# Four-product chains in a transformer trunk: the third and fourth token sums made inside the first chain

## The chip, the cores and the metric

The kernel runs on one core of one Trainium2 chip. Its metric is device time in microseconds, the median of several executions. One execution is also taken with a hardware profiler; its trace is what the views below are read from. The engines are named as the profile names them: PE is TensorE (matmuls), PEld its weight loads, DVE VectorE, ACT ScalarE, POOL GpSimd, SP SyncE. Each works through its own queue in the order in which the program wrote it, and waits at an instruction until the semaphores that it names are there.

## The reference

A trunk of two layers over 512 tokens of width 1024. Layer 0 mixes tokens by dilated windowed attention, layer 1 by a gated recurrence; each is followed by a gated convolutional feed-forward network, with norms before and after. What the change touches is that network:

```
def conv_ffn(x, w_up, conv_w, conv_b, w_down):
    u = causal_dwconv(x @ w_up, conv_w, conv_b)      # w_up: 1024 x 6144, 3 taps
    g, v = u[..., :D_FF], u[..., D_FF:]              # D_FF = 3072
    return (jax.nn.gelu(g, approximate=True) * v) @ w_down
```

Everything is float32. The kernel keeps that accuracy by writing each operand as a high part and a remainder in a shorter format, and by three matmuls for each product (high x high, high x low, low x high; `PASSES`, line 336).

## The kernel before, in words

The feed-forward network (`ffn`, line 674) runs twice. The normed input stands transposed in `hT`, features on partitions, 512 tokens in the free dimension. Weights arrive by SyncE in blocks of 256 columns (`load`, line 280, three buffers `raw`). `pump` (line 245) splits a block into `whi` on ScalarE (line 153) and `wlo` on VectorE (line 154), sixteen units being alive at most. A result tile of 128 features x 512 tokens is a sum over eight blocks of features; `conv` (lines 677 to 686) then does the three taps, the first on ScalarE (line 679) and two on VectorE (line 683), and gelu (line 695, ScalarE) or the product with the gate (line 697, VectorE) follow.

For the gate half of columns 3 to 10 (`SEVEN`, line 39) the product is done as a 2 x 2 block product with seven block products in place of eight (`seven`, line 783). Its operands are blocks of the weights, sums of them (lines 205 and 209 on VectorE, and two additions made by GpSimd DMAs, line 191), blocks of `hT`, and four sums of blocks of `hT` over the two token halves. These four token sums are the same for all eight columns. `token_sums` (line 732) makes them once in each layer: `both` (line 746, the addition at 749) adds the high and low parts of a block of `hT` back together, lines 764, 770, 771 and 777 form the differences and sums, and `parted` (line 757) splits each into two pairs of tiles `T`, by two copies on ScalarE (line 153) and two subtractions on VectorE (line 154).

One column of the seven products is a `chain` (line 813). Its steps are laid into slots by `AT` (line 40): first s1 with the first token sum, then, between quarters of another tile, w11, s4, w12, s2 with the second sum, s3 with the third and a22 with the fourth. Eight chains follow each other 15 slots apart. A chain has two accumulators in PSUM. Between steps they are copied and combined: line 836 (ScalarE) copies the first product aside, which the s4 step needs before it adds to the same bank; lines 840 and 841 (ScalarE) copy both accumulators behind s4, which the w12 step waits for; line 845 (VectorE) finishes the first half of the result ahead of s3, line 848 the second ahead of a22. The chains' matmuls are line 830, those of the other tiles line 340.

The order of work is written out by the program. After each tile or slot `tick` (line 303) runs: it advances the side generators, of which `token_sums` is one, and then pumps one or two weight pieces. A `yield n` lets the generator rest until the nth tick from there. What a slot puts off to later slots (`later`) is emitted ahead of the tick. There are seven ticks between the start of `token_sums` and the first slot of `seven`; in the kernel before it is done by the seventh.

Of the kernel before, what the change touches and what calls it, by code (L numbers as in the profile page):

```python
# [78 lines left out]
def kernel(  # L79
# [38 lines left out]
    def nm(s):  # L118
        uid[0] += 1
        return f"{s}{uid[0]}"  # L120

    def gen(dt=F32, s="g"):
        return gp.tile([P, 512], dt, tag="g", name=nm(s))
# [28 lines left out]
    def split(hi, lo, raw):  # L152
        nc.scalar.activation(hi, raw, AF.Copy)  # L153
        nc.vector.tensor_tensor(lo, raw, hi.bitcast(F32), op=ALU.subtract)  # L154
# [519 lines left out]
    def ffn(layer, hT, post, pre):  # L674
# [31 lines left out]
        for j in range(SEVEN[0]):  # L706
            if j == 1:
                side(token_sums(hT, T))
            if j < SEVEN[0] - 1:
                feat_tiles(2, hT, lambda b, ps: sink(b, ps, j), j == 0)  # L710
            else:
                feat_tiles(1, hT, lambda b, ps: sink(b, ps, j))
                i = chunk()
                feat_tile(i, 0, hT, lambda ps: sink(2, ps, j))
# [17 lines left out]
    def token_sums(hT, T):  # L732

        assert len(sides) == 1
        d = dp.tile([P, 4, D], F32, name=nm("x_kept"))
        nc.gpsimd.dma_start(d, X[0])
        kept.append(d)
        homes = cp.tile([P, 4, D], F32R, tag="x_sb", name=nm("T"))
        homes = [homes[:, n] for n in range(4)]
        homes += [cp.tile([P, D], F32R, tag="gain", name=nm("T"), bufs=2) for _ in range(2)]  # L740
        homes = [[h[:, 0:512], h[:, 512:1024]] for h in homes]
        homes += [[gen(F32R, "T") for _ in range(2)] for _ in range(2)]
        homes = [[h.rearrange("p (k t) -> p k t", k=2) for h in hs] for hs in homes]
        yield 1

        def both(k0, n):
            o = gen(s="B").rearrange("p (k t) -> p k t", k=2)
            hi, lo = (h[:, k0 : k0 + 2, n * 256 : n * 256 + 256] for h in hT)
            tt(o, hi.bitcast(F32), lo.bitcast(F32), op=ALU.add)  # L749
            return o  # L750

        tt = nc.vector.tensor_tensor

        def whole(k0, n):
            return [both(k0 + 2 * k, n) for k in range(2)]

        def parted(n, b):
            for k in range(2):
                split(homes[2 * n][k], homes[2 * n + 1][k], b[k])

        b11, b12 = whole(0, 0), whole(0, 1)
        yield 1
        for k in range(2):
            tt(b11[k], b11[k], b12[k], op=ALU.subtract)
        parted(0, b11)
        yield 1
        b22, b21 = whole(4, 1), whole(4, 0)
        yield 1
        for k in range(2):
            tt(b12[k], b12[k], b22[k], op=ALU.subtract)  # L770
            tt(b22[k], b22[k], b11[k], op=ALU.add)
        yield 1
        parted(1, b22)
        parted(2, b12)
        yield 1
        for k in range(2):
            tt(b21[k], b21[k], b22[k], op=ALU.subtract)
        parted(3, b21)
        T.extend([homes[2 * n], homes[2 * n + 1]] for n in range(4))

    LEFT = {5: ("s1", 1), 1: ("w11", 0), 3: ("s4", 1), 2: ("w12", 0), 6: ("s2", 1), 7: ("s3", 1), 4: ("a22", 1)}

# [647 lines left out]
```

## Time and profile before

| what | us |
| --- | --- |
| median of 3 executions | 1456.36 (1455.86 to 1456.72) |
| the profiled execution, its time | 1456.06 |
| its span, first to last instruction | 1454.3 |
| PE busy | 1436.9 (99%) |
| DVE busy | 971.1 (67%) |
| ACT busy | 736.3 (51%) |
| POOL busy | 178.5 (12%) |
| mean granted TensorE clock | 0.995 of full speed |

A row of a timeline has the start in us from the span's begin, the time from the first start to the last end, engine, line, operation, output and inputs by the program's names (buffer numbers left out), the shape and how many in a row; in brackets the idle time of the engine before it and what ended it. A row of waits has the waiting engine and line, whom it waited for, the total in us, how often, and the longest. Matmuls are pipelined, and their ends are modelled.

### The profile page before, as it was taken

The numbers are of one execution on the slowest core, as the hardware profiler recorded it, in microseconds if no ns is written. First come the engines' busy times: TensorE is split into PE (matmuls) and PEld (weight loads), VectorE is DVE, ScalarE is ACT, GpSimd is POOL, SyncE is SP. The second block draws the span as 40 slices with busy tenths as digits, with TensorE's granted clock in tenths as the row PEclk, the third lists the DMA queues.
The fourth block names the chain that finished last, engine by engine and source line by source line (L and its number), as shares of the span: only waits on it lengthen the run. The fifth ranks groups of instructions, "written<-read, shape, count | busy, mean of one in ns | idle before, by whom it ended". The sixth has DMA issues, their size and how long they took to land.

```text
span 1454.3 us, 20563 instructions
## 1 busy us (share of the span) xinstructions
PE 1436.9 (99%) x7437; PEld 1233.1 (85%) x7437; DVE 971.1 (67%) x2115; ACT 736.3 (51%) x1644; POOL 178.5 (12%) x311
## 2 busy tenths in 40 slices
PE   9999999999999998999999999999998999999998
PEld 7888888888888897989988888888897899988886
DVE  6767747474735979777774348769779777764333
ACT  7656636262615555555543335588454555554331
POOL 0441414040402101101000001000100111000000
PEclk9999999999999999999999999999999999999999
DMA  7653637373726253554452322432333545453201
GB/s 224 207 146 110 172 115 212 100 213 99 217 95 211 87 181 85 142 133 107 137 202 89 114 73 87 131 116 87 117 121 110 146 111 145 123 189 116 87 1 58
DMA packets 142846, 189.66 MB, mean 130 GB/s; under 512 B 9312, under 2 KB 119352, under 8 KB 142232
## 3 DMA queue, kind: packets, MB, share of 16 engines
q1 hardware_dynamic: 114280, 145.48, 31.2%
q0 software_dynamic: 27616, 41.82, 12.0%
q8 instruction: 58, 0.95, 0.3%
q10 hardware_dynamic: 848, 1.05, 0.2%
q14 instruction: 44, 0.36, 0.1%
HBM read 168.83 MB, written 19.49 MB: 129 GB/s over the span
## 4 chain that ended last, share of the span: by engine, by line
PE 85%; DVE 8%; ACT 5%; issue 1%; DVEq 0%; ACTq 0%
PE ps L340 37%; PE acc L340 24%; PE ps L830 11%; PE v L1024 8%; DVE wlo L154 2%; DVE u L683 2%; PE v L954 2%; DVE xb L1233 1%; ACT whi L153 1%; PE O L1175 1%; PE S L1120 1%; PE S L1074 1%; DVE B L749 1%; ACT sig L1254 1%; PE O L340 1%
## 5 line engine op out<-in xcount | busy, mean ns | idle before, releaser
L340 PE MATMUL ps<-hT,whi 128*128 128x512 f32 (+1 forms) x2240 | 646.6, 373 | 0.0
L340 PEld LDWEIGHTS ps<-hT,whi 128*128 128x128 f32 x2240 | 405.0, 189 | 68.8
L340 PE MATMUL ps<-hT,wlo 128*128 128x512 f32 (+1 forms) x1120 | 416.3, 372 | 0.0
L154 DVE TENSOR_TENSOR wlo<-raw,whi 128x512 fp32r<-128x512 f32 x408 | 269.4, 688 | 189.6 <-ACT whi L153 189.6
L153 ACT ACTIVATE whi<-raw 128x512 fp32r<-128x512 f32 x408 | 244.4, 627 | 225.1 <-PE acc L340 118.2
L340 PEld LDWEIGHTS ps<-hT,wlo 128*128 128x128 f32 x1120 | 211.6, 189 | 37.4
L340 PE MATMUL acc<-whi,ahi 128*128 128x512 f32 x512 | 199.6, 390 | 0.0
L340 PE MATMUL acc<-whi,alo 128*128 128x512 f32 x512 | 199.3, 389 | 0.1
L340 PE MATMUL acc<-wlo,ahi 128*128 128x512 f32 x512 | 199.2, 389 | 0.0
L147 ACT ACTIVATE whi<-raw,first_w 128x128 fp32r<-128x128 f32 (+1 forms) x432 | 147.1, 427 | 55.3 <-PE ps L340 30.4
L683 DVE SCALAR_TENSOR_TENSOR u<-ps,cols,u 128x511 f32<-128x511 f32 x192 | 143.6, 748 | 42.6 <-ACT u L679 39.2
L148 DVE SCALAR_TENSOR_TENSOR wlo<-raw,first_w,whi 128x128 fp32r<-128x128 f32 (+1 forms) x432 | 139.6, 391 | 1.9 <-ACT whi L147 1.9
L340 PEld LDWEIGHTS acc<-whi,alo 128*128 128x128 f32 x512 | 96.1, 188 | 20.5 <-DVE alo L154 0.6
L340 PEld LDWEIGHTS acc<-wlo,ahi 128*128 128x128 f32 x512 | 96.1, 188 | 19.8
L340 PEld LDWEIGHTS acc<-whi,ahi 128*128 128x128 f32 x512 | 96.1, 188 | 19.8
L679 ACT ACTIVATE u<-ps,cols 128x512 f32<-128x512 f32 x96 | 73.9, 769 | 70.2 <-DVE ps L845 40.0
L1024 PE MATMUL v<-whi,hT 128*128 128x512 f32 x320 | 102.3, 393 | 0.0
L830 PE MATMUL ps<-T,whi 128*128 128x256 f32 x512 | 92.8, 280 | 0.0
L191 POOL DMA_DIRECT2D raw<-in_ffn_w_up_dram x32 | 41.5, 1489 | 375.1 <-DVE wlo L154 215.6
L383 POOL DMA_DIRECT2D turned<-T x36 | 19.7, 549 | 532.8 <-DVE T L377 529.5
L390 POOL DMA_DIRECT2D ft<-turned x144 | 79.1, 557 | 40.2 <-issue 18.0
L830 PEld LDWEIGHTS ps<-T,whi 128*128 128x128 f32 x512 | 80.1, 189 | 1.6
(196 smaller groups left out, 1609.8 us busy)
## 6 DMA issues: line engine op xcount, KB each, us to landing
raw<-in_ffn_w_up_dram SPq DMA_DIRECT2D x48, 1024.0 KB
raw<-in_attn_w_qkv_dram SPq DMA_DIRECT2D x67, 512.0 KB
raw<-in_ffn_w_down_dram SPq DMA_DIRECT2D x24, 1024.0 KB
raw<-in_ffn_w_up_dram POOLq DMA_DIRECT2D x32, 256.0 KB, 4.6
raw<-in_lru_w_in_dram SPq DMA_DIRECT2D x8, 1024.0 KB
turned<-T POOLq DMA_DIRECT2D x28, 256.0 KB, 2.6
ft<-turned POOLq DMA_DIRECT2D x112, 64.0 KB, 6.0
vrows<-v SPq DMA_DIRECT2D x16, 256.0 KB
```

Of the source, the lines that this page charges most:

```text
L147: nc.scalar.activation(hi[:, k], raw[:, k], AF.Copy, scale=w)
L148: nc.vector.scalar_tensor_tensor(lo[:, k], raw[:, k], w, hi[:, k].bitcast(F32), op0=ALU.mult, op1=ALU.subtract)
L153: nc.scalar.activation(hi, raw, AF.Copy)
L154: nc.vector.tensor_tensor(lo, raw, hi.bitcast(F32), op=ALU.subtract)
L191: nc.gpsimd.dma_start(to, src, accum_op=ALU.add)
L340: mm(dst, l[a], r[b], start=start and n == 0, stop=stop and n == 2)
L390: nc.gpsimd.dma_start(t[32 * c : 32 * c + 32].rearrange("j (b x) -> j b x", b=4), d.rearrange("(b j) (c x) -> c j b x", j=32, c=4)[c],)
L679: nc.scalar.activation(u, ps, AF.Identity, scale=cc[:, j : j + 1], bias=cc[:, 48 + j : 49 + j])
L683: nc.vector.scalar_tensor_tensor(u[:, d:], ps[:, : S - d], wc, u[:, d:], op0=ALU.mult, op1=ALU.add)
L830: mm(y[b][:, 0:256], W[wa][0][:, k, :], right[n](ha, k), start=n in (1, 5) and k == q == 0, stop=k == 3 and q == 2, skip_group_check=True,)
L954: mm(banks[t], hT[a][:, k, t * P : (t + 1) * P], W[b][k % 2][:, 0, :], start=u == n == 0, stop=u == 3 and n == 5,)
L1024: mm(banks[t], hT[a][:, k, t * P : (t + 1) * P], W[b][k % 2][:, 0, :], start=(k, a, b) == (0, 0, 0), stop=(k, a, b) == (KD - 1, 1, 0),)
```

## The change

The generator `token_sums` makes the same four sums by the same operations. Their places differ. The block that only the fourth sum needs (`b21`) is made later, the third sum is split inside the chain, and the fourth is formed and split there too. The list `T` of the tiles is filled after the second sum, ahead of the writes of the last two sums.

```
@@ -764,19 +764,22 @@ def token_sums
             tt(b11[k], b11[k], b12[k], op=ALU.subtract)
         parted(0, b11)
         yield 1
-        b22, b21 = whole(4, 1), whole(4, 0)
-        yield 1
+        b22 = whole(4, 1)
         for k in range(2):
             tt(b12[k], b12[k], b22[k], op=ALU.subtract)
             tt(b22[k], b22[k], b11[k], op=ALU.add)
         yield 1
         parted(1, b22)
+        T.extend([homes[2 * n], homes[2 * n + 1]] for n in range(4))
+        yield 5
         parted(2, b12)
+        yield 4
+        b21 = whole(4, 0)
         yield 1
         for k in range(2):
             tt(b21[k], b21[k], b22[k], op=ALU.subtract)
+        yield 1
         parted(3, b21)
-        T.extend([homes[2 * n], homes[2 * n + 1]] for n in range(4))
```

By ticks: the second sum is formed in the fourth tick (fifth before) and split in the fifth (sixth before). The third sum is split in the tick of the chain's third slot, behind the copy of line 836, which the second slot emits (sixth tick before). The block for the fourth sum is made in the tick of the seventh slot, the sum formed in that of the eighth, and split in that of the ninth (fourth and seventh tick before). The instructions of PE, POOL and SP keep their order; on DVE and ACT the moved ones change places with weight splits and convolutions. Lines behind the change have numbers larger by 3.

More of the change, by code (lines that the diff above doesn't have):

```diff
@@ L766, in token_sums @@
         yield 1
-        b22, b21 = whole(4, 1), whole(4, 0)
-        yield 1
+        b22 = whole(4, 1)
         for k in range(2):
@@ L773, in token_sums @@
         parted(1, b22)
+        T.extend([homes[2 * n], homes[2 * n + 1]] for n in range(4))
+        yield 5
         parted(2, b12)
+        yield 4
+        b21 = whole(4, 0)
         yield 1
@@ L777, in token_sums @@
             tt(b21[k], b21[k], b22[k], op=ALU.subtract)
+        yield 1
         parted(3, b21)
-        T.extend([homes[2 * n], homes[2 * n + 1]] for n in range(4))
     LEFT = {5: ("s1", 1), 1: ("w11", 0), 3: ("s4", 1), 2: ("w12", 0), 6: ("s2", 1), 7: ("s3", 1), 4: ("a22", 1)}
```

## The prediction

> **What bounds the kernel now.** I read the page's busy shares first, then the list of waits of TensorE alone, then the timeline around the longest of them.
>
> ```profile
> span 1454.3 us, 20563 instructions
> ...
> PE 1436.9 (99%) x7437; PEld 1233.1 (85%) x7437; DVE 971.1 (67%) x2115; ACT 736.3 (51%) x1644; POOL 178.5 (12%) x311
> ```
>
> ```profile
> PE ps L830 <- ACT part L836: 8.8, 2, 4.4
> ```
>
> TensorE is the bound, busy for 99% of the span. Of all its listed waits one kind is large: line 830, the products of the chains, waited twice (once in each feed-forward layer) for `part` at line 836, the copy of the first chain's first sum; 8.8 us in all. What moves TensorE is worth its full size, and nothing else is worth anything. So the question is what the moved work does to these two places, and what TensorE waits for next.
>
> I number the slots of the first chain as they are emitted: slot 1 is the product with the first token sum (left operand s1), 2 and 3 are quarters of another tile, 4 is the product of w11, 5 is s4, 6 and 7 quarters, 8 is w12, 9 is s2 (second token sum), 10 to 13 quarters, 14 is s3 (third sum), 20 is a22 (fourth sum). TensorE's timeline, at the starts of slots 2, 4, the end of 4, then 5, 8, 9 and 14; then the end of slot 4, slots 5 and 8 of the second layer:
>
> ```profile
> 564.48 0.63 PE L340 MATMUL ps<-hT,whi 128*128 128x512 f32 x2
> ...
> 567.22 0.40 PE L830 MATMUL ps<-hT,whi 128*128 128x256 f32 x2
> ...
> 568.53 0.28 PE L830 MATMUL ps<-hT,wlo 128*128 128x256 f32 x1
> 573.23 0.50 PE L830 MATMUL ps<-hT,whi 128*128 128x256 f32 x2 [4.42 <-ACT part L836]
> ...
> 579.08 0.40 PE L830 MATMUL ps<-hT,whi 128*128 128x256 f32 x2
> ...
> 580.51 0.40 PE L830 MATMUL ps<-T,whi 128*128 128x256 f32 x2
> ...
> 587.41 0.40 PE L830 MATMUL ps<-T,whi 128*128 128x256 f32 x2
> ...
> 1120.72 0.28 PE L830 MATMUL ps<-hT,wlo 128*128 128x256 f32 x1
> 1125.41 0.80 PE L830 MATMUL ps<-hT,whi 128*128 128x256 f32 x2 [4.42 <-ACT part L836]
> ...
> 1131.95 0.39 PE L830 MATMUL ps<-hT,whi 128*128 128x256 f32 x2
> ```
>
> A chain product takes 1.43 us (579.08 to 580.51), two quarters 2.74 (564.48 to 567.22). Matmuls of this width follow each other by 0.12, so slot 5 was due at 568.65 and came at 573.23: 4.58 us lost. Slots 5 to 7 should then take 1.43 + 2.74 = 4.17 and took 5.85 (573.23 to 579.08): 1.68 more. In the second layer it is 4.57 (1120.84 to 1125.41) and 6.54 - 4.17 = 2.37. The second part is the clock:
>
> ```profile
> 567.18:570.60 3.42, 1.63 (x13) 1.39 (x12) 3.26 (x6) 1.00 (x2) 0.00 (x0) 1.00 0.77 254
> 570.60:574.01 3.41, 0.78 (x6) 0.78 (x7) 3.38 (x7) 3.10 (x7) 0.00 (x0) 1.00 0.20 64
> 574.01:577.42 3.41, 3.41 (x13) 3.00 (x12) 2.71 (x6) 1.49 (x3) 1.28 (x1) 0.50 0.89 299
> ...
> 1120.14:1123.56 3.42, 0.86 (x8) 0.65 (x6) 3.29 (x6) 1.78 (x4) 0.00 (x0) 1.00 0.91 303
> 1123.56:1126.97 3.41, 1.55 (x7) 1.56 (x8) 3.38 (x7) 2.32 (x5) 0.00 (x0) 0.50 0.21 52
> ```
>
> Each row is a stretch of time with its length, the busy time of TensorE, of its weight loads and of three other engines, and the granted clock as the third number from the end. The clock is halved behind a stretch with 0.78 us of TensorE work and behind one with 0.86, and not behind one with 1.63. The two stalls cost 4.58 + 1.68 + 4.57 + 2.37 = 13.20 us in all.
>
> **The change.** It adds and removes no instruction; the order changes on VectorE and ScalarE alone. TensorE's, GpSimd's and SyncE's orders stay. In each layer eight VectorE operations (two sums of line 749, two of 777, four splits at 154) and four ScalarE copies (153) leave the stretch ahead of the copy of line 836 for places behind it. The rows of ScalarE, then VectorE:
>
> ```profile
> 562.51 0.63 ACT L695 ACTIVATE u<-u 128x512 f32<-128x512 f32 x1 [3.04 <-DVE u L683]
> 563.04 2.19 ACT L153 ACTIVATE T<-B 128x512 fp32r<-128x512 f32 x4
> ...
> 565.66 0.76 ACT L679 ACTIVATE u<-ps,cols 128x512 f32<-128x512 f32 x1
> 569.60 1.23 ACT L153 ACTIVATE T<-B 128x512 fp32r<-128x512 f32 x2 [3.18 <-DVE B L777]
> 570.74 2.17 ACT L153 ACTIVATE whi<-raw 128x512 fp32r<-128x512 f32 x4
> 572.82 0.36 ACT L836 ACTIVATE part<-ps 128x256 f32<-128x256 f32 x1
> ...
> 575.93 2.19 ACT L153 ACTIVATE whi<-raw 128x512 fp32r<-128x512 f32 x4 [2.23 <-DVE raw L209]
> ...
> 578.42 0.37 ACT L841 ACTIVATE ps<-ps 128x256 f32<-128x256 f32 x1
> ```
>
> ```profile
> 551.37 2.49 DVE L749 TENSOR_TENSOR B<-hT,hT 128x512 f32<-128x512 f32 x4
> 553.77 1.29 DVE L154 TENSOR_TENSOR wlo<-raw,whi 128x512 fp32r<-128x512 f32 x2
> 554.98 1.53 DVE L683 SCALAR_TENSOR_TENSOR u<-ps,cols,u 128x511 f32<-128x511 f32 x2
> 556.42 0.68 DVE L770 TENSOR_TENSOR B<-B,B 128x512 f32<-128x512 f32 x1
> ...
> 560.88 1.53 DVE L683 SCALAR_TENSOR_TENSOR u<-ps,cols,u 128x511 f32<-128x511 f32 x2
> 563.69 2.50 DVE L154 TENSOR_TENSOR T<-B,T 128x512 fp32r<-128x512 f32 x4 [1.28 <-ACT T L153]
> ...
> 568.88 1.29 DVE L777 TENSOR_TENSOR B<-B,B 128x512 f32<-128x512 f32 x2
> 570.26 1.30 DVE L154 TENSOR_TENSOR T<-B,T 128x512 fp32r<-128x512 f32 x2
> 571.47 1.89 DVE L154 TENSOR_TENSOR wlo<-raw,whi 128x512 fp32r<-128x512 f32 x3
> ...
> 575.21 0.69 DVE L209 TENSOR_TENSOR raw<-raw 128x512 f32<-128x512 f32 x1
> ...
> 583.04 0.42 DVE L845 TENSOR_TENSOR ps<-part,ps 128x256 f32<-128x256 f32 x1
> ```
>
> These give the pitch of a VectorE operation, 0.60 (2.40 for four from 551.37 to 553.77), that of a ScalarE copy, 0.52 (2.08 for four from 570.74 to 572.82), and the old chain: VectorE, full of other work, reaches line 777 at 568.88; ScalarE's split of the fourth sum waits for it until 569.60; four weight copies and line 836 stand behind that split; slot 5 stands behind line 836.
>
> *Slot 5.* I step the new order from 551.37. Until the convolution that began at 560.88 VectorE sheds two sums (1.20) and takes up the two splits of the second sum (1.21) with a wait for ScalarE. That turn-round (convolution, ScalarE's activation, ScalarE's split, VectorE's split) took 2.81 from 560.88 to 563.69, where two convolution steps alone hold the queue 1.45 (554.98 to 556.42), so the wait is 1.36. The convolution begins at 562.25. The activation at 695 follows 1.63 behind, as before (560.88 to 562.51), at 563.88. Then, on ScalarE, one weight copy at +0.53, the convolution's first step at +0.52, four weight copies at +0.76 (565.66), line 836 at +2.08: 567.77, done 0.36 later, at 568.13. Slot 5 is due at 568.65, so this stall goes, with 0.5 us to spare; each microsecond by which I am wrong beyond that comes back in each layer.
>
> *Slot 8, what is late next.* Slot 8 waits for line 841, which ScalarE reaches behind four weight copies, the first of which waits for line 209 on VectorE (575.93, above). Up to line 209 VectorE sheds 1.20 for two sums, 1.21 for two splits of the third sum, 1.38 for line 777 with its wait (568.88 to 570.26), 1.21 for two splits of the fourth: 5.00. It takes up a second turn-round of 1.36, since the weight split behind the next convolution has no splits of sums ahead of it now. Line 209 comes 3.64 earlier, at 571.57; line 841 ended 3.58 behind its start (575.21 to 578.79), now at 575.15, and slot 8 begins 0.05 later (573.18 to 573.23 for the old wait), at 575.20. It is due at 568.65 + 4.17 = 572.82. So a new wait of 2.38 us takes the old one's place. From both sides: nothing, if the turn-rounds are hidden, to 4.6, the old wait, if little of the shed time reaches line 209. I take 2.38, since each term has a row in this very stretch.
>
> *Slots 9, 14 and 20.* The second sum is split at about 559, long before slot 9. Slot 14 waits for the third sum, split by 573.5, and for line 845. From line 209 on VectorE has 16 steps at 0.60 (line 209, two splits of the third sum, four of weights, two sums, one weight split, two of line 777, one weight split, two splits of the fourth sum, line 697) and one convolution of 1.45: 11.05 us, so line 845 begins at 582.62 and ends 0.42 later at 583.04, hardly earlier than before (583.46). TensorE needs it at 575.20 + 8.33 (579.08 to 587.41) = 583.53. It is hidden by 0.5 us; without that cover each microsecond is paid in full, in both layers. The fourth sum is split at 582 and used six slots after slot 14. The four ScalarE copies moved (2.1 us) lie in its waits, of 2.23 at 575.93 and the like.
>
> *Transfers.* No issue is moved in its queue, but two wait for VectorE: SyncE's next loads and GpSimd's addition for the second chain.
>
> ```profile
> 566.82 6.33 SPq L280 DMA_DIRECT2D raw<-in_ffn_w_up_dram  x2
> 575.59 1.28 POOL L191 DMA_DIRECT2D raw<-in_ffn_w_up_dram  x1 [23.99 <-DVE wlo L154]
> DMA to landing us min/median/max: 4.4/4.6/5.8
> ```
>
> The first load goes out 1 us earlier, the addition 3.6 (at 572); landed in 5.8 at the worst it is there at 577.8. The weight split that reads it comes behind line 777, at 580.2, and its copy on ScalarE 0.65 ahead, at 579.6: 1.8 us of cover, behind which line 845 would be late by as much. I cost it at nothing.
>
> *Sum.* First layer: slot 8 begins at 575.20 instead of 579.08, 3.88 saved. Second: the same steps put it 6.55 behind 1120.84, at 1127.39 instead of 1131.95, 4.56 saved. Together 8.44. All that follows is TensorE's own work at 99%, so it reaches the end: 1456.06 (the profiled execution: span 1454.3 and 1.8 around it) - 8.44 = 1447.6 us. The median of the runs, 1456.36, is 0.3 above that execution.
>
> **The rivals.** *The clock falls at the new wait.* For it: a gap of 2.2 us (2.38 less the 0.16 that the last matmul runs past its pitch) leaves 1.2 us of work in a stretch of 3.41, if it lies in one; that is between 0.86, which halved the clock, and 1.63, which didn't. Against it: the stretches stand on a fixed grid of 3.41 us in both layers (574.01 to 1123.56 is 161 of them), the gap may lie across a border, and then neither has so little. Price 1.68 to 2.37 a layer: 1449.3 to 1450.0 for one, 1451.7 for both. [...]
>
> *No new wait.* Both stalls and their clock gone: 1456.06 - 13.20 = 1442.9. It needs line 209 some 2.4 us earlier than I count, both turn-rounds hidden; against it, the one turn-round in these rows was paid.
>
> *It doesn't do what it says.* Line 836 stays late, or slot 8 waits as long as slot 5 did, with the slow clock behind it: 1442.9 + 2 x 4.6 + 1.68 + 2.37 = 1456.1, about 1453.5 if the clock holds once and up to 1457. For it: both slots hang on the same two queues. Against it: 5.0 us of steps leave the queue ahead of line 209.
>
> *Slower.* Slot 14's wait. Line 845 stands behind the weight split that needs GpSimd's addition. It decides from a landing 8.1 us after the issue (572 to 579.6, and the 0.5 of cover), against 5.8 at the worst above; every microsecond past it costs two. At 14 us slot 14 waits 5.9 a layer: 1447.6 + 11.8 = 1459.4, and 1463.5 with the clock's 1.68 and 2.37.
>
> **How the numbers follow.** Forecast (short wait, full clock) 0.42; clock halved in one layer or both 0.32; no new wait 0.10; doesn't do what it says 0.10; slower 0.06. The forecast's own range is 1446 to 1449. For 8 in 10 I take the first three, 0.84, from 1442.5 to 1452.5. What a measurement of this kernel can tell from no change is 0.2%, 2.9 us: the first three cases are faster by more, 0.84; the fourth is the same, 0.10; slower 0.06.
>
> **What would show it.** After: no wait of line 830 for line 836 (now the line with the same copy); a wait of 2 to 3 us for the copy of line 841 at slot 8, released by ScalarE behind line 209; line 209 at 571 to 572 and line 836 ending by 568.7; no wait at slot 14; the span at 1446. Wrong if slot 5 still waits, if slot 8 waits over 4 us, or if line 845 holds slot 14.

## The result, and the profile after

| | before | changed |
| --- | --- | --- |
| median of 6 executions, us | 1456.62 (1455.86 to 1457.72) | 1449.48 (1448.05 to 1451.21) |
| ratio, 95% interval | 1 | 0.9951 (0.9938 to 0.9964) |
| the profiled execution, us | 1456.06 | 1451.21 |
| its span, us | 1454.3 | 1449.4 |

The change saves 7.1 us. The profiled execution of the changed kernel is the slowest of its six; why it is, the clock's rows below tell.

TensorE's list of waits (engine and line, whom it waited for, total us, times, longest) and its timeline at the start of slot 4, the end of 4, the start of 5, the last matmul of slot 7, then slots 8 and 14; the last row is slot 8 of the second layer. Lines behind the change are larger by 3.

```profile
PE ps L833 <- ACT ps L844: 4.5, 2, 2.3
```

```profile
567.43 0.40 PE L833 MATMUL ps<-hT,whi 128*128 128x256 f32 x2
...
568.74 0.28 PE L833 MATMUL ps<-hT,wlo 128*128 128x256 f32 x1
568.86 0.40 PE L833 MATMUL ps<-hT,whi 128*128 128x256 f32 x2
...
572.82 0.39 PE L340 MATMUL ps<-hT,wlo 128*128 128x512 f32 x1
575.48 0.50 PE L833 MATMUL ps<-hT,whi 128*128 128x256 f32 x2 [2.27 <-ACT ps L844]
...
585.44 0.40 PE L833 MATMUL ps<-T,whi 128*128 128x256 f32 x2
...
1125.47 0.50 PE L833 MATMUL ps<-hT,whi 128*128 128x256 f32 x2 [2.28 <-ACT ps L844]
```

Slot 5 follows slot 4 by 0.12 us: the wait of 4.42 us is gone. Slot 8, due at 568.86 + 4.17 = 573.03, begins at 575.48: a new wait, 2.45 us off schedule, 2.27 as the profile counts it. It is the one that the prediction placed there, in both layers. ScalarE and VectorE in the same stretch:

```profile
565.81 2.18 ACT L153 ACTIVATE whi<-raw 128x512 fp32r<-128x512 f32 x4
567.89 0.36 ACT L839 ACTIVATE part<-ps 128x256 f32<-128x256 f32 x1
568.15 0.62 ACT L153 ACTIVATE whi<-raw 128x512 fp32r<-128x512 f32 x1
568.67 1.14 ACT L153 ACTIVATE T<-B 128x512 fp32r<-128x512 f32 x2
572.57 2.19 ACT L153 ACTIVATE whi<-raw 128x512 fp32r<-128x512 f32 x4 [2.75 <-DVE raw L209]
...
575.06 0.37 ACT L844 ACTIVATE ps<-ps 128x256 f32<-128x256 f32 x1
```

```profile
559.45 1.29 DVE L154 TENSOR_TENSOR T<-B,T 128x512 fp32r<-128x512 f32 x2 [1.28 <-ACT T L153]
...
565.27 0.69 DVE L154 TENSOR_TENSOR wlo<-raw,whi 128x512 fp32r<-128x512 f32 x1 [1.28 <-ACT whi L153]
...
571.85 0.69 DVE L209 TENSOR_TENSOR raw<-raw 128x512 f32<-128x512 f32 x1
...
582.93 0.42 DVE L848 TENSOR_TENSOR ps<-part,ps 128x256 f32<-128x256 f32 x1
```

Line 839 ends 0.6 us ahead of slot 5. ScalarE then stands idle for 2.75 us before four weight pieces that need line 209, and the copies for slot 8 stand behind those. Ahead of line 209 VectorE has two waits for ScalarE now, 1.28 each, where it had one.

Stretches of 3.41 us, laid so that the halved ones, which begin at 576.86 and 1126.40 (161 x 3.413 us apart), are whole (stretch, length, busy time of TensorE, of its weight loads, VectorE, ScalarE, GpSimd, then the granted clock, DMA share, GB/s):

```profile
573.44:576.86 3.41, 1.37 (x11) 1.37 (x12) 3.41 (x7) 3.16 (x7) 1.34 (x2) 1.00 0.73 115
576.86:580.27 3.41, 3.41 (x17) 3.32 (x17) 3.38 (x6) 0.87 (x2) 0.00 (x0) 0.50 0.62 77
...
1122.99:1126.40 3.41, 1.14 (x8) 0.94 (x8) 3.41 (x7) 3.38 (x8) 1.97 (x2) 1.00 0.82 159
```

Behind 1.37 and 1.14 us of work the clock is halved for one stretch, in both layers (from 576.86, above, and from 1126.40 to 1129.82, granted clock 0.50). Slot 14 comes 9.96 us behind slot 8, against 8.33 at the full clock: 1.63 us lost there, 1.60 in the second layer. The account of this execution: 13.20 us of old stalls, less 2 x 2.45, less 1.63 and 1.60, is 5.1 us; measured between the two profiled executions 4.85.

### The profile page after: what moved, and what is told of

Its sections match the earlier page's. It is cut to its first block, busy times and chain, and to the rows that moved or that the text cites. A ratio compares the mean times of both kernels' runs of the same rounds, so it can differ in the third digit from the quotient of the medians.

```text
span 1449.4 us, 20563 instructions
## 1 busy us (share of the span) xinstructions
PE 1436.0 (99%) x7437; PEld 1232.4 (85%) x7437; DVE 970.3 (67%) x2115; ACT 734.9 (51%) x1644; POOL 177.6 (12%) x311
## 4 chain that ended last, share of the span: by engine, by line
PE 91%; ACT 4%; DVE 3%; issue 1%; DMA 0%; DVEq 0%; ACTq 0%
PE ps L340 43%; PE acc L340 24%; PE ps L833 11%; PE v L1027 8%; PE v L957 1%; DVE xb L1236 1%; DVE wlo L154 1%; PE O L1178 1%; PE S L1123 1%; ACT whi L153 1%; PE S L1077 1%; ACT sig L1257 1%; PE O L340 1%; PE tr L422 1%; ACT sig L1276 0%
```

## The experiments

All rows are against the kernel before, run beside them.

| kernel | median, us (lowest to highest) | executions | ratio (95%) | waits of the first chain, each layer |
| --- | --- | --- | --- | --- |
| same_again | 1449.66 (1448.10 to 1451.02) | 5 | 0.9953 (0.9940 to 0.9965) | slot 8: 2.3 |
| warm | 1452.52 (1450.71 to 1452.78) | 7 | 0.9972 (0.9961 to 0.9982) | slot 8: 2.3 |
| warm2 | 1448.17 (1448.04 to 1448.96) | 5 | 0.9944 (0.9931 to 0.9958) | slot 8: 0.8 |
| load | 1454.34 (1451.99 to 1454.83) | 10 | 0.9981 (0.9972 to 0.9990) | slot 8: 3.6 |
| third_late | 1453.94 (1452.95 to 1454.31) | 10 | 0.9981 (0.9972 to 0.9990) | slot 5: 3.2 |
| fourth_late | 1450.68 (1449.20 to 1451.59) | 4 | 0.9958 (0.9943 to 0.9973) | slot 8: 2.1 |
| fill | 1450.37 (1449.52 to 1451.31) | 4 | 0.9959 (0.9946 to 0.9973) | slot 8: 2.3 |
| hold | 1446.09 (1445.91 to 1447.04) | 4 | 0.9929 (0.9914 to 0.9944) | slot 14: 1.3 |
| hold_late | 1444.11 (1444.10 to 1444.52) | 4 | 0.9914 (0.9901 to 0.9928) | slot 20: 0.2 |
| fill_hold | 1442.99 (1442.92 to 1443.10) | 4 | 0.9906 (0.9892 to 0.9919) | none |

**The spread of the changed kernel.** The kernel as it is, once more.

> The changed kernel once more, for the spread of its time. Theory 1 (the clock is halved for one stretch of 3.4 us behind the wait of slot 8, in none, one or both layers, by how the gap lies on the grid): the executions fall into three groups, near 1448.1, 1449.5 and 1451.1 us, with mean granted clocks of 0.999, 0.998 and 0.997. Rival (the spread is noise of transfers): times between the groups, and no order by the clock.

The eleven executions of the changed kernel, of both comparisons. The clock is the mean granted clock of an execution; it also holds a stretch at half clock at the very end of the kernel, behind the last matmul (3.0 us in the trace of the kernel before, 2.1 in that of the changed one), where TensorE has no work left, so its third decimal is a coarse count:

| mean clock | executions, us |
| --- | --- |
| 0.999 | 1448.05, 1448.10, 1448.29 |
| 0.998 | 1449.39, 1449.50, 1449.57, 1449.66 |
| 0.997 | 1450.97, 1450.99, 1451.02, 1451.21 |

Three groups, 1.4 and 1.5 us apart, in the order of the clock, and nothing between them. The two profiled ones (both 0.997) have two halved stretches each, one in each first chain. The others have no trace; that the groups are none, one and two halved stretches is read from their times.

**Work inside the wait.** First with twelve products into the unused half of an accumulator's bank, `y[0][:, 256:512]`, ahead of slot 8:

```
             for k in range(4):        # slot 8, first chain only
+                12 x mm(y[0][:, 256:512], whi, hT block, start=True, stop=True)
```

> The changed kernel with twelve products of 256 columns ahead of slot 8, into a half of a bank that is overwritten later and read by nothing before that: 1.4 us of work inside the wait of 2.3 us. Theory 1 (the wait itself costs 2.4 us a layer, and the spread of the changed kernel is the clock, halved for one stretch when TensorE does less than some 1.4 of 3.4 us): no halved stretch, every execution near 1448.1 us. Rival (the clock has its own course, or the spread is transfers): the same three groups from 1448.1 to 1451.1 us, or all of them slower by the added work of 2.9 us.

It failed as an experiment. These products write into the bank that line 844 reads (847 here); they waited for that copy themselves, 2.29 us, and were added behind the wait:

```profile
575.45 2.31 PE L832 MATMUL ps<-hT,whi 128*128 128x256 f32 x12 [2.29 <-ACT ps L847]
```

The median is 3.0 us over the changed kernel's, about the length of 24 products at a pitch of 0.12. They also changed the kernel's result (relative error 0.078), though nothing reads their half before it is overwritten; the bank's other half holds a running sum at that time, but what changed it no run here shows. What it does show: work that comes behind the wait saves nothing. Second, into a bank of their own:

```
+                spare = psum("spare")
+                12 x mm(spare[:, 0:256], whi, hT block, start=True, stop=True)
```

> The changed kernel with twelve products of 256 columns ahead of slot 8 into a bank of their own that nothing reads: 1.4 us of work inside the wait of 2.3 us, which they do not lengthen. Theory 1 (the wait itself costs 2.4 us a layer, and the spread of the changed kernel is the clock, halved behind a stretch of 3.41 us with less than about 1.6 us of TensorE work): no stretch falls below that, no halved clock, every execution near 1448.1 us at a mean clock of 0.999. Rival (the spread has another cause): the three groups from 1448.1 to 1451.1 us as in the changed kernel.

```profile
573.75 1.59 PE L833 MATMUL spare<-hT,whi 128*128 128x256 f32 x12
576.18 0.51 PE L837 MATMUL ps<-hT,whi 128*128 128x256 f32 x2 [0.84 <-ACT ps L848]
```

Slot 8 comes 2.43 us behind the end of slot 7's issue (573.75 to 576.18), as without them, but TensorE is idle for 0.84 only. No stretch of the first chains is halved (3.41 less the gap of 0.84 leaves some 2.6 us of work), all five executions have a mean clock of 0.999, and they lie at 1448.04 to 1448.96, at the fastest group of the changed kernel (1448.05 to 1448.29). The time of the wait and that of the clock behind it are two things: the wait costs 2.4 us a layer in every execution, the clock about 1.5 us in some. The profiled one, 1448.96, is 0.5 to 0.9 above the others. In its trace slot 1 begins at 563.98, against 563.28 and 563.01 in the two of the changed kernel, so most of that arises ahead of the first chain; why is left open.

**VectorE ahead of line 209.** Two more additions, in the tick of slot 2:

```
-        yield 5
+        yield 4
+        ...    # more: a tile that nothing reads
+        for k in range(2):
+            tt(more, b12[k], b22[k], op=ALU.add)
+        yield 1
         parted(2, b12)
```

> The changed kernel with two more additions on VectorE in the tick of the second slot, ahead of line 209, into a tile that nothing reads: 1.2 us in each layer. Theory 1 (slot 8 hangs on line 209 by way of the weight pieces and the copies on ScalarE, without slack): the wait at slot 8 grows from 2.3 to 3.5 us, slot 5 still doesn't wait; 2.4 us over the changed kernel in executions of the same number of halved stretches, so 1450.5 with none, 1452 with one and 1453.5 with two, and two in most of them. Rival (the copies for slot 8 are held by something else, a transfer or the weight pieces' own buffers): the wait stays at 2.3 us, 1448.1 to 1451.1 us.

```profile
573.06 0.68 DVE L209 TENSOR_TENSOR raw<-raw 128x512 f32<-128x512 f32 x1
```

```profile
576.69 0.50 PE L837 MATMUL ps<-hT,whi 128*128 128x256 f32 x2 [3.60 <-ACT ps L848]
```

Line 209 comes 1.2 us later and the wait grows by 1.33, in each layer. The times are 1451.99 to 1452.29 at a clock of 0.998, and 1453.25 to 1454.83 at 0.995 or 0.996: 2.6 us over the changed kernel at 0.998, where 2.4 was expected. No execution is near the 1450.5 expected without a halved stretch; the profiled one, at 0.998, has one, in the second layer. Slot 8 hangs on line 209 without slack.

**The two parts of the change.** The third sum alone late, the fourth as before. The edit is shown against the kernel before:

```
         parted(1, b22)
-        parted(2, b12)
+        T.extend(...)
         yield 1
         for k in range(2):
             tt(b21[k], b21[k], b22[k], op=ALU.subtract)
         parted(3, b21)
-        T.extend(...)
+        yield 3
+        parted(2, b12)
```

> One part of the change alone: the third sum is split in the third slot, the fourth sum made and split ahead of the chain as in the kernel before. Theory 1 (the old stall is the fourth sum: line 839 stands behind ScalarE's split, which stands behind the subtraction on VectorE): slot 5 still waits, some 3.3 us in place of 4.4 in each layer, with a halved clock behind it, and slot 8 waits little or not; 1452 to 1454.5 us. Rival (either part gives half of the gain): 1449.5 to 1451.5 us with a wait under 2.3 us at slot 5.

```profile
PE ps L831 <- ACT part L837: 6.4, 2, 3.2
```

The wait at slot 5 stays, 3.2 of 4.4 us, and the time falls by 2.5 us. And the fourth sum alone late, the third as before (against the changed kernel):

```
         b22 = whole(4, 1)
+        yield 1
...
         parted(1, b22)
+        parted(2, b12)
...
-        yield 5
-        parted(2, b12)
-        yield 4
+        yield 8
         b21 = whole(4, 0)
```

> The other part alone: the third sum is split with the second, ahead of the chain, as in the kernel before; the fourth is made and split in the slots 7 to 9. Theory 1 (VectorE's queue up to line 209 loses a turn-round of 1.4 us and gains the two splits of 1.2 us against the changed kernel): no wait at slot 5, one of 2.0 to 2.3 us at slot 8, the same time as the changed kernel, in its groups from 1447.8 to 1451.1 us. So the third sum's move is worth nothing. Rival (it is worth half): 1452 us or more.

```profile
PE ps L833 <- ACT ps L844: 4.1, 2, 2.1
```

No wait at slot 5, and the changed kernel's time: 1449.20 at a clock of 0.998 and 1450.63 to 1451.59 at 0.997, against 1449.39 to 1449.66 and 1450.97 to 1451.21. The fourth sum's move alone gives the whole gain. Splitting the third sum late as well adds nothing that can be seen: what it takes from VectorE ahead of line 209 (1.2 us) comes back as a turn-round (1.28). The two gains don't add up: by itself the third sum's move does save 2.5 us, since its two splits (1.2 us) then leave the queue ahead of line 777, for which slot 5 still waits.

**The two waits of VectorE filled.** The block for the fourth sum is made while VectorE waits for ScalarE's copy of the second sum, and the fourth sum formed in its next wait:

```
+        b21 = whole(4, 0)
         parted(1, b22)
         T.extend(...)
-        yield 5
-        parted(2, b12)
-        yield 4
-        b21 = whole(4, 0)
         yield 1
         for k in range(2):
             tt(b21[k], b21[k], b22[k], op=ALU.subtract)
-        yield 1
+        yield 4
+        parted(2, b12)
+        yield 6
         parted(3, b21)
```

> The fill and hold kernel without the hold: the operations of the fourth sum stand in VectorE's two waits for ScalarE, its split behind the tenth slot, the weight pieces where the changed kernel has them. Theory 1 (slot 8 hangs on line 209 alone, and line 209 doesn't move): the same wait of 2.3 us at slot 8, line 848 some 3 us earlier, and the same time as the changed kernel, 1448.1 to 1451.1 us in its groups: 2.4 us less work behind line 209 is worth nothing by itself. Rival (the length of VectorE's queue as a whole decides): 1445 to 1447 us.

Four operations that stand behind line 209 in the changed kernel stand ahead of it here, and line 209 begins at the same place:

```profile
558.14 1.29 DVE L749 TENSOR_TENSOR B<-hT,hT 128x512 f32<-128x512 f32 x2
559.51 1.29 DVE L154 TENSOR_TENSOR T<-B,T 128x512 fp32r<-128x512 f32 x2
...
563.97 1.28 DVE L777 TENSOR_TENSOR B<-B,B 128x512 f32<-128x512 f32 x2
565.34 0.69 DVE L154 TENSOR_TENSOR wlo<-raw,whi 128x512 fp32r<-128x512 f32 x1
...
571.92 0.69 DVE L209 TENSOR_TENSOR raw<-raw 128x512 f32<-128x512 f32 x1
...
580.60 0.42 DVE L847 TENSOR_TENSOR ps<-part,ps 128x256 f32<-128x256 f32 x1
```

The splits come at 559.51 and 565.34 here and at 559.45 and 565.27 there: each of the two waits held two operations whole. The copy for slot 14's half (847 here) comes 2.3 us earlier, not the 3 expected, and no time is gained, since the wait at slot 8 is the same 2.3 us. Work taken off VectorE behind the line that TensorE waits for is worth nothing until that wait is gone.

**The wait at slot 8 taken away.** The pump is held in the slots 3, 4 and 5 of the first chain, so that the pieces that wait for line 209 come behind the copies of line 844:

```
             if m in steps or m >= end:
+                state["hold"] = m in (2, 3, 4)
                 slot(...)
```

> No weight piece is split in the third, fourth and fifth slot of the first chain, so that ScalarE reaches the copies for slot 8 without standing behind the piece that waits for line 209. Theory 1 (what is left is one VectorE queue that is late: take away the wait at slot 8 and slot 14 waits for line 848): no wait at slot 8, a new one of about 1.4 us at slot 14 in each layer (line 848 ends near 582.7, slot 14 is due at 581.4), 1442.9 + 2.7 = 1445.6 us, no halved clock. Rival (line 848 has room, the prediction's half microsecond of cover was too small): no wait, 1442.9 us.

```profile
582.61 0.51 PE L833 MATMUL ps<-T,whi 128*128 128x256 f32 x2 [1.27 <-DVE ps L848]
```

The wait moves from slot 8 to slot 14, 1.27 us in each layer, 1446.09 in place of 1445.6. This wait cost somewhat more than the idle time that the profile lists, as at slot 5 before (4.42 idle, 4.58 late): slot 14 begins 1.43 behind its place (the last product ahead of it at 580.96, and a pitch of 0.22), and its first three products take 0.11 longer than usual, 1.54 in all. The cover of half a microsecond that the prediction gave line 848 was no more than that. With the fourth sum four slots later as well (`yield 8` for `yield 4`):

> The same, and the fourth sum made four slots later, behind line 848. Theory 1: line 848 ends near 579 against a need at 581.4, no wait at slot 8 or 14, no halved clock, all 13.2 us of the two old stalls gone: 1442.9 us, span near 1441. Rival (part of the gain of the change goes elsewhere, so that the rest isn't to be had by these two slots): over 1445 us.

No wait at slot 8 or 14, but 1444.11, 1.2 us over what was expected. It is a wait at slot 20 for line 851, which now stands behind the fourth sum: 0.25 us idle in each layer.

```profile
589.97 0.28 PE L833 MATMUL ps<-hT,wlo 128*128 128x256 f32 x1
590.49 0.50 PE L833 MATMUL ps<-T,whi 128*128 128x256 f32 x2 [0.25 <-DVE ps L851]
```

Slot 20 was due at 590.09, 0.12 behind the product ahead of it, and is 0.40 late. Its first three products take 0.10 longer than usual, and so do those of the slot ahead, 0.09. That is 0.59 a layer, the whole 1.2 us. Last, the hold and the filled waits together:

> Weight pieces held as in the hold kernel. The block for the fourth sum is made ahead of the splits of the second sum, and the fourth sum formed one tick later, each of them in one of VectorE's two waits for ScalarE of 1.28 us; its split is done behind the tenth slot. Theory 1 (the two waits of VectorE are idle time that holds two operations each): line 209 begins where it does in the changed kernel, 571.9 by its trace, no wait at slot 8 or 14: 1442.9 us. Rival (the two operations delay what stands behind them): line 839 comes 1.2 us later and slot 5 waits about 0.5 to 1 us, 1444 to 1446 us.

```profile
span 1441.2 us, 20561 instructions
...
PE 1432.7 (99%) x7437; PEld 1230.1 (85%) x7437; DVE 970.2 (67%) x2115; ACT 733.8 (51%) x1644; POOL 177.5 (12%) x311
```

TensorE waits nowhere in the chains. 1442.99 us is 13.6 below the kernel before and 6.5 below the changed one, within 0.1 of the time worked out from the two old stalls. It is the best version found.

## Why the prediction was right

The time forecast was 1447.6, the median measured 1449.48. That lies in the range of 1442.5 to 1452.5, which takes in the rivals, but above the 1446 to 1449 that the prediction gave its own forecast case: the waits came as forecast, and the clock mostly did not. Step by step:

- *Slot 5.* Line 836 was to end 0.5 us ahead of need; it ends 0.6 ahead (568.25 against 568.86). third_late and fourth_late show the cause: the fourth sum's split in ScalarE's queue.
- *Slot 8.* A new wait of 2.38 us was forecast, measured as 2.45 on the same count. Line 209 was to come 3.64 us earlier; against the operation that starts the stretch (551.37 before, 551.57 now) it comes 3.56 earlier. load shows the mechanism from the other side: line 209 1.2 us later, the wait 1.33 longer.
- *Slots 9, 14, 20.* No wait, as forecast. Line 848 ends at 583.35, 0.46 us ahead of where slot 14 would stand at the full clock; 0.5 was forecast, and hold shows the edge. Behind a halved stretch slot 14 comes later (585.44 in this trace) and the cover is larger. At the full clock the trace of warm2 shows it: the same line ends at 584.04 and slot 14 begins at 584.62, without a wait.
- *Transfers.* Cost nothing in the first chains, as taken: VectorE goes from line 209 to line 848 without a wait.
- *The sum.* Where the clock held, the changed kernel took 1448.05 to 1448.29. That is 0.5 above the 1447.6, of which 0.3 is the distance of the profiled execution from the median that the prediction named.
- *The clock.* Here a term was mis-sized, and it is the one that parts forecast and median. The prediction gave the full clock 0.42 and a halved one in either layer 0.32. Of eleven executions three had the full clock and eight didn't; by their groups, 12 of their 22 first chains were halved. The price was on the high side: 1.4 and 1.5 us between the groups, 1.60 and 1.63 in the trace, against 1.68 to 2.37 taken. The 2.37 was the price of two halved stretches, not of one: behind the last row of stretches in the prediction a second one follows at a clock of 0.50 (shown in the last section). What failed is the chance. The rows of before left open what comes behind a stretch with between 0.86 and 1.63 us of work; in the runs 1.53 was still followed by half clock and 1.55 no longer (last section). As an estimate from these two rows, take 1.54, their middle: a gap of 2.27 us leaves less than that in some stretch if 1.87 of it or more lies in one: (3.41 - 2.27 + 2 x 0.40) / 3.41 = 0.57 of all positions, and 12 of 22 is 0.55. That they agree so well is in part luck: the sum takes every position as equally likely, the executions are few, and the second layer's position hangs on the first's. The median is the case with one halved layer, which the prediction priced at 1449.3 to 1450.0.
- *The other rivals.* "No new wait" didn't come, and its time, 1442.9, is the one that fill_hold reached. Slot 14's wait, the slower one, didn't come, though it is the next to show when slot 8's is taken away; there it comes from the length of VectorE's queue, not from a late transfer.

## What to carry to other kernels

When a stall hangs on a queue shared with other work, step the new order operation by operation with the pitches of that very stretch, until the next place where the bound engine waits: here that gave the old stall's end, the new one's place and its size to 0.1 us. Moving work behind a wait pays only until that wait is gone (the fourth sum's move took the whole of it, and the third's added nothing), and idle time made by a hand-over between two engines held other work for nothing (fill: two operations in each wait of 1.28 us, line 209 at 571.92 against 571.85). Price a short idle gap of TensorE with the clock behind it, as a chance: here 2.27 us idle brought 1.4 to 1.6 us more in 12 of 22 first chains, counted from the groups of times.

## What the runs showed of the hardware

The clock was halved behind stretches in which TensorE was far from idle. These are stretches of 3.41 us that themselves ran at the full clock, in the order of TensorE's busy time: 1.37 (the changed kernel), 1.43 (load) and 1.53 (third_late) were followed by half clock, 1.55 (load) and 1.63 (before) were not.

```profile
567.28:570.70 3.41, 1.53 (x13) 1.33 (x11) 3.31 (x6) 2.29 (x5) 0.00 (x0) 1.00 0.81 277
```

```profile
571.54:574.95 3.41, 1.55 (x7) 0.94 (x5) 3.38 (x7) 1.17 (x3) 1.28 (x1) 1.00 0.70 245
574.95:578.36 3.41, 1.67 (x14) 1.68 (x15) 3.41 (x6) 2.92 (x7) 1.27 (x1) 1.00 0.95 118
```

The first row is of third_late, the clock halved behind it (0.50 from 570.70 to 574.11); the other two are of load, where a gap of 3.60 us lies across two stretches and neither is followed by half clock. The busy times rest on modelled ends of matmuls, and 1.53 and 1.55 are one row each.

Two stretches that were themselves at half clock were followed by half clock, though they held 1.55 us of work and more. In the second layer of the kernel before, the stretch from 1123.56 had 1.55 us, and the next one was halved too:

```profile
1126.97:1130.38 3.41, 3.41 (x13) 2.93 (x13) 2.71 (x5) 2.27 (x5) 1.28 (x1) 0.50 0.79 265
```

In third_late the stretch from 570.70 to 574.11 had 2.07 us, and the products behind it still followed each other by 0.21 in place of 0.12:

```profile
574.13 0.63 PE L831 MATMUL ps<-hT,whi 128*128 128x256 f32 x2
574.55 0.41 PE L831 MATMUL ps<-hT,wlo 128*128 128x256 f32 x1
```

Behind the halved stretches of before that were filled, 3.41 us of work from 574.01 and from 1126.97, the clock was at 1.00 again. No row here of a stretch at half clock has a value between 2.07 and 3.41.

The clock fell at 574.01 and 1123.56 in the kernel before and at 576.86 and 1126.40 in the changed one, 549.55 us apart in both, 161 times 3.413. Gaps of 2.27 us had half clock behind them where they left 1.37 and 1.14 us of work in a stretch, and one of 3.60 had not where it left 1.55 and 1.67 in two. The same kernel took 1448.1, 1449.5 or 1451.1 us; that the gaps' place among the stretches makes the difference is an inference, since only the slowest group has traces.
